# Cached keys stored transposed by page, pages loaded by SyncE at addresses from registers, eight page numbers per register load

## The chip, the cores and the metric

The kernel runs on one core of one Trainium2 chip. The metric is device time in microseconds (us), the lower the better: the median of three runs. A profiled execution of the same program is read beside it.

The engines are named as the profile names them: PE (TensorE, matmuls) with PEld (its weight loads), ACT (ScalarE), DVE (VectorE), POOL (GpSimd) and SP (SyncE, which here only issues DMAs).

## The reference, cut to what matters

One layer of a decoder trunk, for 512 prompt tokens and 8 sample groups of 4 tokens that share the weights. In words and lines of the reference:

```
mod = silu(c) @ w_ada + b_ada                       # six modulation vectors
h   = rmsnorm(x, norm1) * (1 + sc1) + sh1
bg, cg, xin, q, kc, vc, ks, vs, kw, vw, nsa_g, merge_g = split(h @ w_in)
y_a = (bg * conv3(cg * xin)) @ w_out_conv
# sample group: past = 1024 positions in 8 pages of 128, named by page_table
rows(cache) = cache[page_table] + the group's new rows
kc, vc = compress(rows(cache_cmp))    # gelu(blocks of 32 rows @ w1) @ w2, stride 16
o_b = g0 * attend(q, kc, vc) + g1 * attend(q, top 16 blocks of rows(cache_sel))
      + g2 * attend(q, window: cache_win + new rows)       # each with a distance penalty
x   = x + g1 * ((ga * y_a + gb * (o_b @ w_o_nsa)) @ w_out)
x   = x + g2 * SwiGLU(rmsnorm(x, norm2) ...);   y = rmsnorm(x, norm_f)
```

`cache_cmp` and `cache_sel` are 80 physical pages of 128 rows; a row holds the keys and the values of four heads, 512 numbers in all. `cache_win` holds 512 such rows for each of the 8 sample groups ("batches" below). The three attention branches of a sample batch need for their scores the keys with the channel on the partitions, and for their weighted sums the values with the position on the partitions.

## The kernel before, in words

Everything is float32. A product of two float32 matrices is made of three passes over PE: both operands are split into a rounded high part and a rest (weights by `split`, L225: ACT copies the high part at L231, DVE subtracts at L232), and `mm3` (L235) multiplies high by high (L236), high by rest (L237) and rest by high (L238). A token batch of 544 columns is cut in halves of 288 and 256.

Weights come as slabs of 1 MB, loaded by SP (`slab`, L222) into a ring of three buffers, in the order in which they are used. In the first stage the function `queue` ties each SP DMA behind the one issued before it, so that SP works through one list written by hand: page table, first compression weights, the small constants `hp`, the pages of batch 0, and so on. Elsewhere a scheduler that estimates durations places each engine's instructions; an engine then works through its own list strictly in that order.

The stages, in order:

1. **Compression** (to about 151 us of the trace). For each batch `b` and `v` = 0 (keys) or 1 (values), that is `n` = 0 to 15 with `b = n // 2`: `cmp_gather` loads the 8 pages of a batch (one register load of a page number and one DMA each, L464 and L465), `cmp_split` makes the high part on ACT (`xh`, L494) and the rest on DVE (`xl`, L495) of two blocks of 128 x 1024, `cmp_M` runs 48 matmuls (L507 to L509) into the PSUM tile `phi`, `cmp_finish` adds and applies Gelu (`t` on ACT at L515, two DVE additions, `h` on ACT at L519). The splits of step `n + 1` are written behind the finish of step `n`. Between the steps stand the slabs of the modulation weights (`mod_slab`, PE at L285) and the norm of the tokens. Batch 0 is loaded in two goes, keys first, the values behind the second compression weights. `wake` (L539) runs matmuls on constants whose result nobody uses.
2. **Linears for keys, values, gates and queries** (to about 305 us). The queries are written to DRAM (`q_dr`, L733) to be rearranged.
3. **Samples** (about 305 to 526 us). `sample_gen` runs once for each pair of batches: scores on the compressed keys, importance, then `branch` for the selected keys and `branch` for the window. Its instructions are laid between the matmuls of `fill_gen`, 108 quarters of linears with 12 matmuls each, which are needed anyway: `yield k` in `sample_gen` hands over to `k` quarters. One pair yields 27 quarters, four pairs and the start of each 112.

   Within a pair: `gather` loads the selected pages by one indirect DMA per batch on POOL (L820, 2 MB each, tile `sraw`), with row numbers `ixs` that DVE works out from the page table at the end of stage 1; the window comes by two POOL DMAs of 1 MB (`wraw`). The loaded keys have the position on the partitions, so `key_T` (L881) turns them on PE against an identity matrix, four transposes of 128 x 128 into a PSUM tile, and ACT or DVE copies that out (`kt`, L183 or L185). Then `ss` (L900) multiplies queries by keys, `softmax_part` (L810) adds the bias table, ACT takes the exponential (L911), DVE normalises (L917), PE turns the probabilities (`pt`, L924), they are copied out (`pts`), and `sacc` (L931) sums the values.
4. The merge of both mixers, the prompt's attention, the output projection and the FFN (to the end).

The order of a branch in the code, cut:

```
kts = key_T(raw, 0, 0); yield 1; kts += key_T(raw, 0, 1); yield 1
for q4 in range(k): ss matmuls (4 quads); softmax_part; next key_T's with yields
exp, normalise; yield 4
transposes pt and copies pts; yield 1
sacc matmuls
```

Of the kernel before, what the change touches and what calls it, by code (L numbers as in the profile page):

```python
# [142 lines left out]
def build(tc, a, o):  # L143
# [262 lines left out]
    pti = mp.tile([128, 64], I32, name="pti")  # L406
    ptf = mp.tile([128, 64], F32, name="ptf")
    pm_ = mp.tile([128, 64], F32, name="pm_")
    fidx = mp.tile([128, 8], F32, name="fidx")
    queue(lambda: sync.dma_start(pti, a["page_table"].rearrange("(x b) g -> x (b g)", x=1).broadcast_to([128, 64])))  # L410
# [39 lines left out]
    def cmp_gather(b, vs=(0, 1)):  # L450


        if b not in gb_:
            if b == 6:
                gb_[b] = [raw_tile("gt6").rearrange("p (j w) -> p j w", j=4) for _ in range(2)]
            elif b in (2, 5, 7):
                gb_[b] = [gat.tile([128, 8, 512], F32, tag="gt", bufs=1, name=nm("gt"))]
            else:
                gb_[b] = [hpool.tile([128, KC * NT], F32, tag="h" + "hl"[b in (1, 4)], bufs=1, name=nm("gt"))[:, 0:4096].rearrange("p (j w) -> p j w", j=8)]
        cs = slice(256 * vs[0], 256 * vs[-1] + 256)  # L460

        def page(pg):
            t = gb_[b][pg // 4][:, pg % 4, cs] if b == 6 else gb_[b][0][:, pg, cs]
            r = sync.value_load(pti[0:1, b * 8 + pg:b * 8 + pg + 1], min_val=0, max_val=N_PHYS - 1)  # L464
            return sync.dma_start(t, ccv[bass.ds(r, 1)].rearrange("n p w -> (n p) w")[:, cs])  # L465
# [87 lines left out]
    for n in range(16):
# [41 lines left out]
        if n == 15:  # L595
            mk8 = tsm[:, 19:27].rearrange("p (x m) -> p x m", x=1).broadcast_to([128, 8, 8])
            with tc.issue_after(last_lo[0].ins):
                dve.tensor_copy(ptf, pti)
                dve.tensor_mul(pm_.rearrange("p (b x) -> p b x", b=8), ptf.rearrange("p (b x) -> p b x", b=8), mk8)
                dve.tensor_reduce(fidx, pm_.rearrange("p (b x) -> p b x", b=8), axis=AX.X, op=ALU.add)  # L600
                dve.tensor_scalar(ixs, fidx, 16.0, tsm[:, 2:3], ALU.mult, ALU.add)
# [879 lines left out]
```

## Time and profile before

| | before |
|---|---|
| median of 3 runs | 1327.63 us (1326.82 to 1328.21) |
| the profiled execution, its own time | 1327.7 us |
| its span, first to last instruction | 1325.9 us |
| mean granted TensorE clock | 0.988 |
| DMA moved | 191.39 MB, mean 144 GB/s |
| stage 1 up to | 151.5 us |
| stage 2 up to | 305.0 us |
| stage 3 up to | 526.5 us |

The span is what the trace shows; 1.8 us of the execution's own time lie outside it. The stage ends are read from the trace's timeline of PE by the first matmul of the next stage.

How to read what follows. A group row gives the line of the code, the engine, the operation, `out<-in` by the program's names, partitions x elements, a count, and times. A row of the waits view gives who waited for whom, the sum, the number of waits, and the longest. A row of the windows view gives a stretch of the span, its length, the busy time of each engine in it with the number of its instructions, the granted TensorE clock as a share of full speed, the mean share of the DMA engines, and GB/s. A row of the timeline gives a start, a duration, the instruction, and in brackets how long its engine stood idle before it and who released it. `SPq` and `POOLq` are the sequencers that issue DMAs.

### The profile page before, as it was taken

Reading aid. Unit: us, or ns where it says so; the run is one execution under the profiler, and the core shown is the slowest. Engines: PE = TensorE matmul, PEld = TensorE weight load, DVE = VectorE, ACT = ScalarE, POOL = GpSimd, SP = SyncE. Lnnn points to the kernel's source line nnn. Section 1 sums busy time; section 2 is a strip of 40 time slices with the busy share of each in tenths; the row PEclk is TensorE's granted clock in tenths of the full one; section 3 lists DMA queues with packets and bytes.
Section 4 is the critical chain, followed back from the end, with each engine's and each line's share of the span. In section 5 each row is a group of like instructions: output and inputs, shape, how many; then the busy total and the mean of one; then the engine's idle time right before and its main releaser. Section 6 shows DMA issues by size and latency. Waiting matters only on the chain.

```text
span 1325.9 us, 26272 instructions
## 1 busy us (share of the span) xinstructions
PE 1293.4 (98%) x10950; PEld 1208.0 (91%) x10950; DVE 641.5 (48%) x1553; ACT 542.8 (41%) x1070; POOL 54.8 (4%) x105
## 2 busy tenths in 40 slices
PE   6999999999999999999999999999999999999997
PEld 4889999998898998998778778999999999999996
DVE  3347632344355454336668576667333333333335
ACT  4346543333232335126677676445323222222223
POOL 1000120001111010001000000000000000000000
PEclk8899999999999999999999999999999999999998
DMA  5975146663755543834536334331123122122211
GB/s 179 360 251 172 68 145 228 223 210 108 278 210 211 223 159 129 210 120 136 150 128 200 108 103 179 127 128 65 64 70 122 64 96 96 56 88 88 88 65 68
DMA packets 43398, 191.39 MB, mean 144 GB/s; under 512 B 4980, under 2 KB 12532, under 8 KB 26904
## 3 DMA queue, kind: packets, MB, share of 16 engines
q1 hardware_dynamic: 40832, 163.52, 36.6%
q0 software_dynamic: 2448, 26.19, 5.1%
q8 instruction: 86, 1.41, 0.4%
q14 instruction: 32, 0.26, 0.1%
HBM read 174.49 MB, written 23.54 MB: 149 GB/s over the span
## 4 chain that ended last, share of the span: by engine, by line
PE 91%; DMA 3%; SPq 2%; DVE 1%; issue 1%; ACT 1%; POOL 0%; POOLq 0%; DVEq 0%; ACTq 0%
PE lin L236 19%; PE lin L237 19%; PE lin L238 19%; PE dn L238 3%; PE dn L236 3%; PE dn L237 3%; PE acc L1164 3%; PE ptp L1170 3%; PE phi L507 2%; PE modp L285 2%; PE phi L508 2%; PE phi L509 2%; DMA wraw<-in_cache_win 2%; PE kt L881 2%; PE sp L1139 1%
## 5 line engine op out<-in xcount | busy, mean ns | idle before, releaser
L232 DVE TENSOR_TENSOR wl<-raw,wh 128x1024 fp32r<-128x1024 f32 (+1 forms) x148 | 178.7, 1207 | 261.4 <-ACT wh L231 260.9
L231 ACT ACTIVATE wh<-raw 128x1024 fp32r<-128x1024 f32 (+1 forms) x148 | 154.9, 1047 | 332.6 <-PE lin L237 238.7
L236 PE MATMUL lin<-h_h,wh 128*128 128x288 f32 x976 | 286.8, 294 | 0.0
L238 PE MATMUL lin<-h_h,wl 128*128 128x288 f32 x976 | 281.4, 288 | 0.0
L237 PE MATMUL lin<-h_l,wh 128*128 128x288 f32 x976 | 280.9, 288 | 0.0
L237 PE MATMUL lin<-h_lo,wh 128*128 128x288 f32 (+1 forms) x672 | 193.9, 289 | 0.0
L238 PE MATMUL lin<-h_hi,wl 128*128 128x288 f32 (+1 forms) x672 | 193.4, 289 | 0.0
L236 PE MATMUL lin<-h_hi,wh 128*128 128x288 f32 (+1 forms) x672 | 192.7, 287 | 0.0
L236 PEld LDWEIGHTS lin<-h_h,wh 128*128 128x128 f32 x976 | 183.8, 188 | 9.5 <-issue 8.3
L237 PEld LDWEIGHTS lin<-h_l,wh 128*128 128x128 f32 x976 | 183.9, 188 | 0.4
L238 PEld LDWEIGHTS lin<-h_h,wl 128*128 128x128 f32 x976 | 183.7, 188 | 0.3
L236 PEld LDWEIGHTS lin<-h_hi,wh 128*128 128x128 f32 x672 | 126.8, 189 | 0.0
L237 PEld LDWEIGHTS lin<-h_lo,wh 128*128 128x128 f32 x672 | 126.5, 189 | 0.2 <-DVE h_lo L361 0.2
L238 PEld LDWEIGHTS lin<-h_hi,wl 128*128 128x128 f32 x672 | 126.1, 188 | 0.0
L236 PE MATMUL dn<-f_hi,wh 128*128 128x256 f32 (+1 forms) x352 | 101.7, 289 | 0.0
L238 PE MATMUL dn<-f_hi,wl 128*128 128x256 f32 (+1 forms) x352 | 101.5, 288 | 0.0
L237 PE MATMUL dn<-f_lo,wh 128*128 128x256 f32 (+1 forms) x352 | 101.1, 287 | 0.0
L507 PE MATMUL phi<-xh,wph 128*128 128x256 f32 x256 | 77.4, 302 | 9.8 <-ACT xh L494 9.8
L508 PE MATMUL phi<-xl,wph 128*128 128x256 f32 x256 | 75.9, 296 | 3.1 <-DVE xl L495 3.1
L1146 ACT ACTIVATE P<-P,nms 128x512 f32<-128x512 f32 (+3 forms) x128 | 70.7, 555 | 19.6 <-DVE nms L1145 18.7
L509 PE MATMUL phi<-xh,wpl 128*128 128x256 f32 x256 | 75.1, 294 | 0.0
L1145 DVE CUSTOM_DVE_ANT_0 P<-sp,ta 128x512 f32<-128x512 f32 (+3 forms) x128 | 57.6, 482 | 30.1 <-PE sp L1133 22.4
(349 smaller groups left out, 2381.6 us busy)
## 6 DMA issues: line engine op xcount, KB each, us to landing
raw<-in_wt SPq DMA_DIRECT2D x98, 1024.0 KB, 4.9
gt<-in_cache_cmp SPq DMA_DIRECT2D x56, 256.0 KB, 3.2
wraw<-in_cache_win POOLq DMA_DIRECT2D x8, 1024.0 KB, 8.7
out_new_win_sample<-in_cache_win SPq DMA_DIRECT2D x8, 512.0 KB, 5.8
out_new_win_sample<-in_cache_win SPq DMA_DIRECT2D x8, 504.0 KB
raw<-in_wt SPq DMA_DIRECT2D x4, 768.0 KB, 4.2
xT<-in_xT SPq DMA_DIRECT2D x1, 2176.0 KB
x<-in_xT SPq DMA_DIRECT2D x1, 2176.0 KB
```

What stands on the lines that cost most here:

```text
L231: act.activation(oh, view, AF.Copy)
L232: dve.tensor_sub(ol, view, oh.bitcast(F32))
L236: pe.matmul(p, lhsT=wh[:, k, :], rhs=xh, start=start, stop=False)
L237: pe.matmul(p, lhsT=wh[:, k, :], rhs=xl, start=False, stop=False)
L238: pe.matmul(p, lhsT=wl[:, k, :], rhs=xh, start=False, stop=stop)
L507: pe.matmul(ps_, lhsT=w_h, rhs=mh, start=(ch == 0 and s == 0), stop=False)
L508: pe.matmul(ps_, lhsT=w_h, rhs=ml, start=False, stop=False)
L509: pe.matmul(ps_, lhsT=w_l, rhs=mh, start=False, stop=(ch == 7 and s == 1))
L1145: dve.tensor_tensor_reduce(out=t[:, 0:n], in0=sps[br], in1=t_dist[:, 512 - n:512], scale=-hs, scalar=3e38, op0=ALU.add, op1=ALU.min, accum ...
L1146: act.activation(t[:, 0:n], t[:, 0:n], AF.Exp, scale=-1.0, bias=nms[:, c:c + 1], accum_out=sums[:, c:c + 1])
L1164: pe.matmul(acc[br * 64:br * 64 + 64, :], lhsT=vtok[br][:, j, g * 64:(g + 1) * 64], rhs=pts_[br], start=(j == 0), stop=False)
L1170: pe.transpose(tp[:, r * 128:(r + 1) * 128], P[br, r][:, 128 * j:128 * j + 128], ident)
```

## The change

- **The page table** is loaded to one partition (`ptr`, 1 x 64) instead of to all 128 (`pti`).
- **Register loads**: `pages_of` reads the eight page numbers of a batch with one instruction into eight registers and issues eight DMAs behind it, in place of one load, one check and one DMA for each page.
- **Batch 0** of the compression pages comes whole, ahead of the second compression weights. From batch 3 on a batch's pages are put in SP's list ahead of the modulation slab of the same step, at `n` = 1, 3, 5, 8, 11 in place of 2, 4, 6, 8, 11, and the token tile `xT` is asked for at `n` = 2 in place of 1. `wake` runs three matmuls where it ran two, once.
- **Cached keys transposed**: on the host, each page of `cache_sel` and each window is laid out so that the key half has the channel on the rows and the position in the columns; the value half stays. `key_T` with its transposes and copies is gone, `ss` reads the loaded tile. The bias tables take plain position order.
- **Selected pages** are loaded by SP, 16 page DMAs for a pair, instead of by POOL's indirect DMA: the first pair's ahead of the query linears, the next pair's right behind the selected branch's weighted sum. The window is asked for by SP as the pair starts. `sraw` has three buffers where it had two. The row numbers `ixs` are not worked out any more.
- **The yields** of a pair are 4, 3, 6, 2, 5, 5, 2, 2, 2 (31 quarters) where they were 27 in all, so four pairs with their starts hold 128 places for the 108 quarters.

The diff, cut:

```diff
+    def pages_of(b, cache, dst):
+        src = a[cache].rearrange("(n p) w -> n p w", p=128)
+        ld, regs = queue(lambda: nc.values_load_multi_w_load_instructions(ptr[:, b * 8:b * 8 + 8], [mybir.EngineType.SP], ...), lambda r: r[0][-1])
         for pg in range(8):
-            queue(lambda: page(pg))
+            queue(lambda: sync.dma_start(dst(pg), src[bass.ds(regs[pg], 1)].rearrange("n p w -> (n p) w")))
...
-    cmp_gather(0, (0,))
+    cmp_gather(0)
     phi_load(1)
-    cmp_gather(0, (1,))
...
-    wake(2)
+    wake(3)
...
-        for s_ in AHEAD.get(n, ()):
-            adas.append(slab("ada", s_))
-        if n == 1:
+        if n in (1, 3, 5, 8, 11):
+            cmp_gather({1: 3, 3: 4, 5: 5, 8: 6, 11: 7}[n])
+        if n in AHEAD:
+            adas.append(slab("ada", AHEAD[n]))
+        if n == 2:
             queue(lambda: sync.dma_start(xT.rearrange("p k n -> p (k n)"), a["xT"]))
-        if n in (2, 4, 6, 8, 11):
-            cmp_gather({2: 3, 4: 4, 6: 5, 8: 6, 11: 7}[n])
...
+    def gather(bp):
+        rows_of[bp] = [srp.tile([128, 8, 512], F32, tag="sraw", bufs=3, name=nm("sraw")) for _ in range(2)]
+        for b2 in range(2):
+            pages_of(2 * bp + b2, "cache_sel", lambda pg: rows_of[bp][b2][:, pg, :])
+    gather(0)
...
-        sraw = gather(bp)
+        sraw = rows_of.pop(bp)
+        wt = srp.tile([128, 2, 2048], F32, tag="sraw", bufs=3, name=nm("wraw"))
         for b2 in range(2):
+            sync.dma_start(wt[:, b2], a["cache_winT"][b0 + b2])
...
-            kts = key_T(raw, 0, 0)
-            yield 1
-            kts += key_T(raw, 0, 1)
-            yield 1
             for q4 in range(k):
-                for (b2, gp, rows), kt in zip(quads, kts):
-                    pe.matmul(p[rows, :], lhsT=qbd[:, b0 + b2, gp, :], rhs=kt, start=True, stop=True)
+                for b2, gp, rows in quads:
+                    pe.matmul(p[rows, :], lhsT=qbd[:, b0 + b2, gp, :], rhs=keys(b2, gp, q4), start=True, stop=True)
...
-            yield 4
+            yield wait
...
-        yield from branch(sraw, 8, [bs[:, 0:512], bs[:, 512:1024]], 64, 1, True)
-        wt = srp.tile([128, 2, 4, 512], F32, tag="sraw", bufs=2, name=nm("wraw"))
-            pool.dma_start(wt[:, b2], a["cache_win"][b0 + b2].rearrange("(p j) w -> p j w", j=4))
-        yield 6
-        yield from branch(wr, 4, [t_win], 96, 2, False)
+        yield from branch(..., 8, [bs[:, 0:512], bs[:, 512:1024]], 64, 1, True, 6)
+        if bp < 3:
+            gather(bp + 1)
+        yield 5
+        yield from branch(..., 4, [t_win], 96, 2, False, 5)
```

Four places where the instructions stand otherwise. The first is SP's list at the start. `gt_2` is batch 0's tile of pages, `raw_1` and `raw_3` are the two slabs of compression weights, `ISA` rows are register arithmetic. Before:

```order
L410 DMA pti_122<-in_page_table 128x64
L222 DMA raw_1_144<-in_wt 128x2048
L474 DMA hp_134<-in_hp 128x264
L464 TENSOR_LOAD pti_122
L464 ISA x2
L465 ISA
L465 DMA gt_2_147<-in_cache_cmp 128x256
L464 TENSOR_LOAD pti_122
L464 ISA x2
L465 ISA
L465 DMA gt_2_147<-in_cache_cmp 128x256
```

After:

```order
L406 DMA ptr_121<-in_page_table 1x64
L220 DMA raw_1_140<-in_wt 128x2048
L468 DMA hp_130<-in_hp 128x264
L448 TENSOR_LOAD ptr_121
L450 ISA
L450 DMA gt_2_143<-in_cache_cmp 128x512
L450 ISA
L450 DMA gt_2_143<-in_cache_cmp 128x512
```

Before, a page half costs five instructions; after, a whole page costs two, and one load stands ahead of eight pages.

The second place is ACT's list around the steps `n` = 1 to 3. `xh_31` and `xh_33` are the high parts for `n` = 2, `xh_42` and `xh_44` (after: `xh_43` and `xh_45`) for `n` = 3, all from batch 1's tile `gt_4`; `t1_29` belongs to the finish of `n` = 1. Before:

```order
L515 ACTIVATE t1_29_675<-phi_26_619,pbias_136 128x256
L494 ACTIVATE xh_31_681<-gt_4_311 128x1024
L519 ACTIVATE h1_30_679<-t1_29_675 128x252
L494 ACTIVATE xh_33_685<-gt_4_311 128x1024
L494 ACTIVATE xh_42_772<-gt_4_311 128x1024
L494 ACTIVATE xh_44_776<-gt_4_311 128x1024
```

After (`xh_19` and `xh_21` are the high parts for `n` = 1, `t1_17` the finish of `n` = 0):

```order
L487 ACTIVATE xh_19_342<-gt_2_143 128x1024
L487 ACTIVATE xh_21_346<-gt_2_143 128x1024
L423 ACTIVATE wph1_127<-raw_3_169 128x512 x4
L508 ACTIVATE t1_17_336<-phi_15_284,pbias_132 128x256
L512 ACT_TABLE_LOAD
L512 ACTIVATE h1_18_340<-t1_17_336 128x252
L487 ACTIVATE xh_31_433<-gt_4_172 128x1024
L487 ACTIVATE xh_33_437<-gt_4_172 128x1024
L487 ACTIVATE xh_43_549<-gt_4_172 128x1024
L487 ACTIVATE xh_45_553<-gt_4_172 128x1024
L181 ACTIVATE kcs0_89<-ph2_28_423 128x2x63
L508 ACTIVATE t1_29_427<-phi_26_371,pbias_132 128x256
```

The splits for `n` = 1 have moved ahead of the finish of `n` = 0, and those for `n` = 2 and 3 ahead of the finish of `n` = 1. The split for `n` = 6 (`xh_80`), which before stands behind the finish of `n` = 5, has likewise moved ahead of it.

The third place is ACT's list around `n` = 7 and 8. `t1_105` is the finish of `n` = 7, `xh_107` and `xh_109` the high parts for `n` = 8 from batch 4's tile. After:

```order
L508 ACTIVATE t1_93_976<-phi_91_921,pbias_132 128x256
L512 ACTIVATE h1_94_980<-t1_93_976 128x252
L508 ACTIVATE t1_105_1055<-phi_103_1002,pbias_132 128x256
L487 ACTIVATE xh_107_1061<-gt_62_673 128x1024
L487 ACTIVATE xh_109_1065<-gt_62_673 128x1024
```

Before, the same `xh_107` stands two rows ahead of `t1_105`; now it stands behind it.

The fourth place is PE's list near the end of the samples: `pt` and `sacc` of the last pair's selected branch, `ss` of its window, and `lin`, the fill. Before, fill follows the transposes `pt`:

```order
L924 MATMUL pt_759_6405<-ident_66,S_726_6198 128x128 x4
L924 MATMUL pt_761_6412<-ident_66,S_726_6198 128x128 x4
L236 MATMUL lin_767_6426<-h_h_2076,wh_765_6422 128x288
L237 MATMUL lin_767_6426<-h_l_2077,wh_765_6422 128x288
L238 MATMUL lin_767_6426<-h_h_2076,wl_766_6423 128x288
```

After, with the last fill matmul as the first row:

```order
L236 MATMUL lin_688_5918<-h_h_1553,wl_686_5889 128x256
L876 MATMUL ss_695_5992<-wraw_654_5717,qbd_95 32x512
L895 MATMUL pt_689_5944<-ident_66,S_676_5859 128x128 x4
L895 MATMUL pt_691_5951<-ident_66,S_676_5859 128x128 x4
L876 MATMUL ss_695_5992<-wraw_654_5717,qbd_95 32x512 x3
L902 MATMUL sacc_675_5858<-sraw_619_5364,pts_690_5949 32x128 x2
```

Behind these rows no fill stands any more: the rest of the selected sum, the window's `pt`, `ptx`, `sacc` and `ot` follow one upon the other up to the linears of the merge. SP's list has the 16 page DMAs of `gather(0)` right behind the last query slab and ahead of the writes to `q_dr` and of the next two slabs; the 16 of each later pair stand ahead of one to two slabs of the fill and wait for the `sacc` that frees their buffers.

More of the change, by code (lines that the diff above doesn't have):

```diff
@@ L206, in build, with queue @@
     ordered, last_q = [True], [None]
-    def queue(f):
+    def queue(f, ins=lambda r: r):
         if not ordered[0]:
@@ L403, in build @@
     v_dr = [dr.tile([128, 1024], F32, name=f"v_dr{j}") for j in range(2)]
[L406 to L410, printed above, removed]
+    ptr = mp.tile([1, 64], I32, name="ptr")
+    ptv = a["page_table"].rearrange("(x b) g -> x (b g)", x=1)
+    queue(lambda: sync.dma_start(ptr, ptv))
     p0 = ExitStack()
@@ L445, in build, with cmp_gather @@
     gat = mkpool(gst, "gat", side="right")
-    ccv = a["cache_cmp"].rearrange("(n p) w -> n p w", p=128)
     gb_ = {}
[L450 to L465, printed above, removed]
-        for pg in range(8):
-            queue(lambda: page(pg))
+    def pages_of(b, cache, dst):
+        src = a[cache].rearrange("(n p) w -> n p w", p=128)
+        ld, regs = queue(lambda: nc.values_load_multi_w_load_instructions(ptr[:, b * 8:b * 8 + 8], [mybir.EngineType.SP], min_val=0, max_val=N_PHYS - 1, skip_runtime_bounds_check_because="a page table names pages of the cache"), lambda r: r[0][-1])
+        for pg in range(8):
+            queue(lambda: sync.dma_start(dst(pg), src[bass.ds(regs[pg], 1)].rearrange("n p w -> (n p) w")))
+    def cmp_gather(b):
+        if b == 6:
+            ts = [raw_tile("gt6").rearrange("p (j w) -> p j w", j=4) for _ in range(2)]
+        elif b in (2, 5, 7):
+            ts = [gat.tile([128, 8, 512], F32, tag="gt", bufs=1, name=nm("gt"))]
+        else:
+            ts = [hpool.tile([128, KC * NT], F32, tag="h" + "hl"[b in (1, 4)], bufs=1, name=nm("gt"))[:, 0:4096].rearrange("p (j w) -> p j w", j=8)]
+        gb_[b] = ts
+        pages_of(b, "cache_cmp", lambda pg: ts[pg // 4][:, pg % 4] if b == 6 else ts[0][:, pg])
     xst = ExitStack()
@@ L595, in build @@
         if n == 15:
[L596 to L601, printed above, removed]
             xst.close()
@@ L813, in small @@
         return smp.tile([128, w_], F32, tag=f"sm_{n}", bufs=2, name=nm(n))
[L816 to L822 removed]
     def sample_gen(bp):
         b0 = 2 * bp
[L827 removed]
+        sraw = rows_of.pop(bp)
+        wt = srp.tile([128, 2, 2048], F32, tag="sraw", bufs=3, name=nm("wraw"))
+        for b2 in range(2):
+            sync.dma_start(wt[:, b2], a["cache_winT"][b0 + b2])
         quads = [(b2, gp, slice(b2 * 64 + gp * 32, b2 * 64 + gp * 32 + 32)) for b2 in range(2) for gp in range(2)]
@@ L869, in sample_gen, with branch @@
         for jh in range(2):
[L870 to L872 removed]
+            pool.tensor_tensor(bs[:, jh * 512:(jh + 1) * 512].rearrange("p (s k) -> p s k", s=8),
+                               t_sel[:, jh * 512:(jh + 1) * 512].rearrange("p (s k) -> p s k", s=8),
+                               mk[:, jh * 8:jh * 8 + 8].rearrange("p (s y) -> p s y", y=1).broadcast_to([128, 8, 64]), op=ALU.add)
         dve.tensor_scalar_mul(px[:, 0:63], px[:, 0:63], G[:, 0:1])
[L875 to L885 removed]
+        yield 3
         acc = acc_ps(nm("sacc"))
[L889 removed]
+        def branch(keys, vals, nj, tables, xo, br, first, wait):
             S = smp.tile([128, 1024], F32, tag="S", bufs=1, name=nm("S"))
```

77 lines of the change are left out of this document (30 added, 47 removed).

## The prediction

> **What bounds the kernel now.** I read the page first.
>
> ```profile
> span 1325.9 us, 26272 instructions
> PE 1293.4 (98%) x10950; PEld 1208.0 (91%) x10950; DVE 641.5 (48%) x1553; ACT 542.8 (41%) x1070; POOL 54.8 (4%) x105
> PEclk8899999999999999999999999999999999999998
> ```
>
> PE is busy for 98% of the span, so a change pays only if it takes matmuls off PE, removes one of its few idle stretches, or keeps its clock up. The clock row is low in the first two slices only. I therefore cut the span by windows, small ones at the start, where the change moves loads.
>
> ```profile
> 11.80:17.40 5.60, 0.06 (x2) 0.04 (x1) 0.67 (x3) 1.15 (x2) 0.00 (x0) 0.71 0.59 200
> 17.40:28.50 11.10, 10.09 (x82) 9.51 (x82) 5.76 (x11) 3.55 (x7) 0.00 (x0) 0.69 0.54 174
> 28.50:33.00 4.50, 1.97 (x9) 1.35 (x10) 2.09 (x4) 3.72 (x5) 0.00 (x0) 0.80 0.81 237
> 33.00:40.70 7.70, 7.70 (x47) 7.56 (x45) 0.51 (x1) 0.00 (x0) 0.00 (x0) 0.68 0.91 325
> 40.70:44.00 3.30, 0.92 (x5) 0.65 (x5) 2.23 (x4) 3.20 (x5) 0.00 (x0) 1.00 0.89 294
> 44.00:48.20 4.20, 4.20 (x47) 3.68 (x46) 3.00 (x3) 1.64 (x3) 0.00 (x0) 0.60 0.81 296
> 48.20:75.80 27.60, 27.60 (x300) 25.53 (x299) 7.76 (x18) 7.85 (x15) 0.00 (x0) 1.00 1.01 390
> 75.80:80.00 4.20, 1.13 (x6) 0.91 (x5) 2.50 (x4) 3.75 (x9) 0.00 (x0) 0.88 0.94 331
> 80.00:82.50 2.50, 2.50 (x37) 1.80 (x36) 2.29 (x4) 2.15 (x4) 0.00 (x0) 0.53 0.96 338
> 82.50:151.50 69.00, 69.00 (x651) 65.55 (x650) 50.20 (x132) 43.59 (x83) 0.31 (x4) 1.00 0.42 138
> 305.00:526.50 221.50, 216.17 (x2060) 197.69 (x2059) 110.78 (x291) 77.70 (x135) 26.12 (x55) 1.00 0.49 187
> 526.50:1325.90 799.40, 788.22 (x6413) 737.27 (x6410) 398.92 (x995) 334.01 (x713) 7.43 (x11) 1.00 0.34 110
> ```
>
> The compression stage has four holes, before 17.4, at 28.5, 40.7 and 75.8 us, and behind each the clock is down (0.69, 0.68, 0.60, 0.53): a hole is paid twice. The sample stage (305 to 526.5) idles for only 5.3 us; what can be had there is PE's own work. Nothing in the last 800 us is touched, and I leave them as they are. The waits of PE name the holes:
>
> ```profile
> PE phi L507 <- ACT xh L494: 9.8, 4, 5.5
> PE phi L508 <- DVE xl L495: 3.1, 4, 0.9
> PE kt L881 <- DMA wraw<-in_cache_win: 2.7, 3, 1.3
> ```
>
> Four waits for the split of cached pages and three for the window.
>
> **The first matmul.** SP's own rows, the chain's row of the page table, and ACT and PE at the start:
>
> ```profile
> L464 SPq TENSOR_LOAD <-pti x72: 263/268/476, 5.0 to 120.5; - x72
> L465 SPq DMA_DIRECT2D gt<-in_cache_cmp x72: 332/333/1219, 6.0 to 121.3; - x72
> 6.01 8.26 SPq L465 DMA_DIRECT2D gt<-in_cache_cmp  x8
> 16.25 2.00 ACT L494 ACTIVATE xh<-gt 128x1024 fp32r<-128x1024 f32 x2 [4.64 <-DMA gt<-in_cache_cmp]
> 17.36 0.58 PE L507 MATMUL phi<-xh,wph 128*128 128x256 f32 x1 [5.54 <-ACT xh L494]
> ```
>
> Eight half pages take 8.26 us to issue, a period of about 1.1 us, of which the DMA instruction is 0.33. The last is issued at 14.3 and the split starts at 16.25, 2.0 later. After the change a page costs the DMA and one or two small register operations, I say 0.4 us; eight are out 3.2 us after the first. They are whole pages now, 2 MB, and at the 390 GB/s of the window 48.20 to 75.80 that takes 5.4 us: from 6.3, with 2.0 for the landing, ready at 13.7. That is 2.6 ahead of 16.25. One register load for eight numbers is not in the trace: between one load as now (0.27) and eight of them (2.1). I take the short end, since one instruction replaces eight, and with the bounds of the transfer get **-2.6 (-4 to -1)**. [...]
>
> The clock in 17.4 to 28.5 is 0.69, so 3.4 us are lost there. The hole before shrinks from both sides (one more `wake` matmul, the earlier data), to some 3 us: I take **-1.5 (-3.4 to 0)**.
>
> **The three holes that go.** At 28.5 the split of batch 0's values stands behind the finish of step 0, because the values come in a second go. After, the split's two ACT rows stand ahead of that finish, and the tile is loaded with the keys. Idle 4.50 - 1.97 = 2.5, and 7.70 us at 0.68 lose 2.5: **-5.0 (-5.6 to 0)**. At 40.7 the split for step 2 stands behind the finish of step 1 in ACT's list:
>
> ```profile
> 40.80 0.47 ACT L515 ACTIVATE t<-phi,pbias 128x256 f32<-128x256 f32 x1 [8.57 <-PE phi L509]
> ```
>
> ACT had idled 8.57 us before it, and the split could have run there. After, batch 1's four splits stand ahead. Idle 3.30 - 0.92 = 2.4, and 4.20 at 0.60 lose 1.7: **-4.1**. At 75.8 the same for step 6: idle 3.1, 2.50 at 0.53 lose 1.2: **-4.3**. The cover for all three is that the pages land in time. In bytes, batch 3's pages (needed by step 6) stand after 12 MB of SP's list, some 31 us at 390 GB/s, so at about 37; step 6 starts near 60. Batch 1's end after 6.2 MB, at about 22 us, and step 2 starts near 28.
>
> **One new hole.** The split of batch 4 for step 8 now stands behind the finish of step 7 on ACT. It is the shape of the holes at 40.7 (4.1) and 75.8 (4.3), so **+4.0 (0 to +5)**.
>
> **The transposes.**
>
> ```profile
> L881 PE MATMUL kt<-ident,sraw x128: 270/273/331, 309.8 to 489.3; 128*128 128x128 f32 x128
> L881 PE MATMUL kt<-ident,wraw x64: 270/272/301, 341.4 to 514.6; 128*128 128x128 f32 x64
> 309.91 1.90 PE kt L881 x16
> 317.01 0.87 PE kt L881 x8
> ```
>
> The 270 ns are a pipelined matmul's full length; what PE is held for is read from the chain of waits, 1.90 for 16 or 0.87 for 8, that is 0.119 or 0.109 each. PE is full here, so all 192 count: 22.8 (20.9 to 22.8). **-22.8**. The copies on ACT and DVE that fall away, the index arithmetic on DVE and POOL's DMAs lie beside PE: 0. `ss` reads its 512 columns as four pieces of 128 where it read one; the `phi` matmuls, which read pieces of 32 columns, run 300 in 27.60 us with the rest of that window, so 0. The window's load is asked for at the start of the pair, and the three waits of the third view go: **-2.7**. Nothing waits next: `ss` has its keys long before, and the four score blocks still wait for DVE's `mk` and POOL's table as before.
>
> **The end of the samples.** 128 places are handed over for 108 quarters, so the fill ends within the fourth pair, and what follows is a chain. The end before:
>
> ```profile
> 518.56 0.72 ACT L911 ACTIVATE S<-S,m 128x512 f32<-128x512 f32 x1 [0.96 <-DVE m L909]
> 520.31 0.48 DVE L917 TENSOR_SCALAR S<-S,f 128x512 f32<-128x512 f32 x1
> 521.93 0.60 PE L924 MATMUL pt<-ident,S 128*128 128x128 f32 x4
> 522.01 1.06 ACT L231 ACTIVATE wh<-raw 128x1024 fp32r<-128x1024 f32 x1 [2.33 <-PE lin L237]
> 522.57 0.69 DVE L185 COPY pts<-pt 128x512 f32<-128x512 f32 x1 [1.62 <-PE pt L924]
> 523.31 1.08 PE L931 MATMUL sacc<-wraw,pts 128*32 128x128 f32 x32 [0.67 <-DVE pts L185]
> 523.36 1.28 ACT L1022 ACT_TABLE_LOAD   x1
> 524.65 0.66 ACT L1022 ACTIVATE ga<-ga 128x544 f32<-128x544 f32 x1
> 525.53 0.33 PE L953 MATMUL ot<-ident,ob 128*128 128x128 f32 x1 [0.92 <-ACT ob L950]
> 526.49 0.72 PE L236 MATMUL lin<-yin_hi,wh 128*128 128x288 f32 x3
> ```
>
> From `pt` at 521.93 to the next linear at 526.49 are 4.6 us, in which PE works about 2.7. After, ACT's list behind the last fill is: split 1.06, copy 0.4, table 1.28, sigmoid 0.66, copy of `pts` 0.6, table 1.28, exponential 0.72; then from its end to the normalised `S` 1.5, and `pt`, `pts`, `sacc`, the output 3.5 to 4.2: some 11.7 us. PE has in it, beside the 2.7, the selected branch's `pt`, `sacc` and one `ss` that stood among the fill: 1.2 + 2.2 + 1.0, so 7. Idle 4.7 against 1.9 makes +2.8, and a hole of that length costs 1.2 to 2 us of clock, as after 75.8 and 40.7. **+4.5 (+2 to +9)**; the far end is the hole with both table loads bare and the clock down for longer.
>
> **SP's queue.** The 16 pages of a later pair wait for the `sacc` that frees their buffers, and a slab of the fill stands behind them. Between the `sacc` and the use of that slab I count 304 matmuls; at 799.40 / 6413 = 0.125 each that is 38 us, less the slab's landing and split, 7: 31 us of cover for pages of 0.4 each, 6.4. So 0, and 0 (to +3) for the `q_dr` writes behind `gather(0)`, since `linear` has further buffers.
>
> **Sum**: -2.6 - 1.5 - 5.0 - 4.1 - 4.3 + 4.0 - 22.8 - 2.7 + 4.5 = -34.5. The profiled execution's own time is 1327.7 (span 1325.9 and 1.8 outside), within 0.1 of the median 1327.63, so **1293 us**.
>
> **The rivals.**
>
> A: The pages come no faster, and the holes of the first stage stay. The windows 11.80 and 17.40 moved 200 and 174 GB/s while pages were the load; if that is the rate of small pieces and not of their issue, batch 0 whole needs 10 us and more, and the splits wait for data instead of for ACT's list. Then only transposes, window, the new hole, the end of samples and at most the first term are left: -22.8 - 2.7 + 4.0 + 4.5 - 2.6 = -19.6, so **1308**. [...] Against it, the window 48.20 moved 390 GB/s with pages in the mix. Chance 0.12.
>
> B: The two new holes don't show, as step 8 finds other work of PE and the exponential is off the end: -34.5 - 8.5 = -43, so **1284.5**. For it, PE has modulation matmuls about step 8, and in the trace of before step 4 crosses without a hole. Chance 0.12.
>
> C, slower: SP's one queue. The pages of a later pair hold the slabs back. It decides where 16 pages take over 31 us, 1.9 each; each further us is paid three times (pairs 2 to 4). To be slower than before it must make up 34.5, 11.5 each time, so 2.7 us a page; at 2.75 it is 3 x 13 = 39, **1332**. The nearest row:
>
> ```profile
> 47.79 14.30 SPq L465 DMA_DIRECT2D gt<-in_cache_cmp  x8
> ```
>
> Eight issues took 14.3, 1.8 each, where the DMA engines were full (390 GB/s); in the sample stage they are at 0.49. Chance 0.04.
>
> **How the numbers follow.** My forecast has 0.72, A 0.12, B 0.12, C 0.04. The forecast's own range, from the bounds of the terms (first term +1.6, clock +1.5, end +4.5 upward; new hole -4, end -2.5, clock -1.9 downward, not all at once), is 1286 to 1300. B lies just below and A above; 1281 to 1305 leaves out A, C and the edges, below 2 in 10. What a measurement of this kernel can tell from no change is 0.2%, 2.7 us; every case but C is far under that. Faster 0.95, same 0.02 (C near its point of balance), slower 0.03.
>
> **What would show it.** In the profile after: the first `phi` near 14.7; no wait of `phi` for `xh` at steps 1, 2 and 6, one of 2 to 3 us at step 8 with a low clock behind it; no `kt`; 16 pages issued in 6 to 8 us; PE's busy time lower by about 25; stage 3 shorter by about 21, a hole of several us near its end; the stretch behind it unchanged at 799. It is wrong if the holes of stage 1 stay with ACT waiting for `gt`, if `lin` waits for splits that wait for `raw`, or if the register load takes several us.

## The result, and the profile after

| | before | after |
|---|---|---|
| median | 1327.29 us (4 runs, 1326.82 to 1328.21) | 1294.78 us (4 runs, 1293.24 to 1294.94) |
| the profiled execution, its own time | 1327.7 us | 1294.94 us |
| its span | 1325.9 us | 1293.2 us |
| mean granted TensorE clock | 0.988 | 0.992 |
| PE busy | 1293.4 us | 1269.4 us |

The ratio is 0.9752, with a 95% interval of 0.9735 to 0.9769. The forecast was 1293, in a range of 1281 to 1305. The total is met within 2 us, but by luck: two misses of opposite sign cancel, as the stages show. I cut both spans at the same three instructions: the first linear behind the compression, the first score of the samples (`sx`), and the first matmul on `yin`, the merge's input, which ends the samples. The middle two stretches of before:

```profile
151.50:301.50 150.00, 150.00 (x1230) 148.74 (x1228) 51.50 (x87) 54.18 (x89) 16.80 (x24) 1.00 0.55 190
301.50:526.49 224.99, 219.66 (x2099) 201.04 (x2097) 112.00 (x291) 79.02 (x137) 26.79 (x56) 1.00 0.49 187
```

After, with the starts of the first stage and the holes in rows of their own (the columns are those of the windows in the prediction):

```profile
8.00:13.30 5.30, 3.77 (x38) 1.79 (x38) 1.59 (x5) 2.92 (x6) 0.00 (x0) 1.00 1.06 415
13.30:22.30 9.00, 8.12 (x62) 7.90 (x66) 7.19 (x9) 4.89 (x7) 0.00 (x0) 0.81 1.03 405
22.30:30.00 7.70, 7.70 (x106) 7.32 (x98) 4.26 (x7) 5.96 (x7) 0.00 (x0) 1.00 1.04 407
30.00:71.80 41.80, 41.78 (x431) 39.36 (x423) 17.99 (x35) 17.38 (x36) 0.00 (x0) 1.00 0.82 326
71.80:74.70 2.90, 0.54 (x2) 0.34 (x3) 1.93 (x4) 2.88 (x5) 0.00 (x0) 1.00 0.00 0
74.70:80.00 5.30, 5.30 (x94) 4.34 (x95) 5.10 (x10) 4.18 (x11) 0.00 (x0) 1.00 0.39 140
...
133.86:284.60 150.74, 150.74 (x1231) 149.43 (x1230) 51.54 (x88) 53.87 (x90) 15.68 (x22) 1.00 0.58 198
284.60:487.18 202.58, 199.08 (x1905) 182.07 (x1905) 97.84 (x268) 66.84 (x114) 13.94 (x42) 0.99 0.57 210
487.18:491.26 4.08, 0.63 (x7) 0.41 (x4) 1.99 (x4) 2.91 (x6) 0.00 (x0) 0.86 0.32 106
491.26:497.00 5.74, 5.74 (x24) 5.74 (x25) 4.39 (x7) 0.00 (x0) 0.00 (x0) 0.50 1.03 261
```

| stage | before | after | measured | forecast |
|---|---|---|---|---|
| compression, to the first linear | 151.5 | 133.9 | -17.6 | -13.5 |
| linears, to the first `sx` | 150.0 | 150.7 | +0.7 | 0 |
| samples, to the first matmul on `yin` | 225.0 | 202.6 | -22.4 | -21.0 with the row below |
| the rest | 799.4 | 806.0 | +6.6 | |
| sum | 1325.9 | 1293.2 | -32.7 | -34.5 |

The first stage gave 4 us more than I said. The transposes and the window's wait were to bring -25.5 in the samples; -22.4 came there and +6.6 went behind them, so the end of the samples cost 9.7 (what is left when those 25.5 are taken as right), where I said 4.5 and 9 at most. PE's waits in the changed kernel:

```profile
PE lin L235 <- DVE yin_lo L265: 3.5, 1, 3.5
PE phi L500 <- ACT xh L487: 3.0, 2, 1.5
PE pt L895 <- DVE S L888: 2.5, 1, 2.5
PE phi L501 <- DVE xl L488: 1.7, 2, 0.9
```

Of the four waits for `xh` two are left, the first matmul and step 8; the window's is gone. The second row from the bottom is the hole that I forecast at the end of the samples. The first row I had not forecast at all. The timeline of DVE and PE there:

```profile
486.30 0.80 DVE L931 COPY o_s<-ot 64x32 f32<-64x32 f32 x4 [3.00 <-PE ot L925]
487.12 0.68 DVE L966 COPY nco<-ncp 18x512 f32<-18x512 f32 x1
487.18 0.63 PE L234 MATMUL lin<-yin_hi,wh 128*128 128x288 f32 x3
489.89 0.68 DVE L966 COPY nco<-ncp 18x512 f32<-18x512 f32 x1 [2.09 <-DMA out_new_conv_sample<-nco]
491.26 0.61 PE L235 MATMUL lin<-yin_lo,wh 128*128 128x288 f32 x1 [3.45 <-DVE yin_lo L265]
```

DVE's second copy into `nco` (the convolution's new state on its way to DRAM) waits for the DMA that empties the first, and `yin_lo`, which the merge's first linear needs, stands behind it. In the kernel before, seven of the eight `yin_lo` stood ahead of that second copy:

```profile
527.33 4.51 DVE L267 TENSOR_TENSOR yin_lo<-yinf,yin_hi 128x544 fp32r<-128x544 f32 x7
531.78 0.67 DVE L994 COPY nco<-ncp 18x512 f32<-18x512 f32 x1
```

After, PE idles 3.45 us, and then 5.74 us run at a clock of 0.50. Behind the first hole, the wait for `S`, the clock is down as well:

```profile
482.00:487.18 5.18, 4.13 (x54) 3.07 (x53) 1.70 (x7) 1.73 (x4) 0.00 (x0) 0.67 0.19 75
```

From 476 to 497 us PE idles 6.95 us, where it idled 2.1 from 520 to 530 before; the two stretches of low clock lose about 1.4 and 2.9 us (work at 0.67 and at 0.50), where before the clock was 1.00. Counted in this way, the end costs about 9.1 us more.

At the start, the rows of SP, ACT and PE that answer to those of before, with the register load of eight page numbers:

```profile
L448 SPq TENSOR_LOAD <-ptr x16: 525/529/1740, 2.0 to 431.5; - x16
2.99 4.03 SPq L450 DMA_DIRECT2D gt<-in_cache_cmp  x8
12.20 3.90 ACT L487 ACTIVATE xh<-gt 128x1024 fp32r<-128x1024 f32 x4 [2.37 <-DMA gt<-in_cache_cmp]
13.31 0.39 PE L500 MATMUL phi<-xh,wph 128*128 128x256 f32 x1 [1.54 <-ACT xh L487]
```

The first page is asked for at 2.99, not at 6.0, because the narrow page table is there by 2.0; the first `phi` comes 4.05 us earlier, where I said 2.6.

### The profile page after: what moved, and what is told of

The parts are those of the page before. It is cut to its first block, busy times and chain, and to the rows that moved or that the text cites. A ratio compares the mean times of both kernels' runs of the same rounds, so it can differ in the third digit from the quotient of the medians.

```text
span 1293.2 us, 25776 instructions
## 1 busy us (share of the span) xinstructions
PE 1269.4 (98%) x10760; PEld 1187.6 (92%) x10760; DVE 627.1 (48%) x1525; ACT 531.3 (41%) x1048; POOL 40.9 (3%) x89
## 4 chain that ended last, share of the span: by engine, by line
PE 96%; DVE 2%; ACT 1%; DMA 1%; SPq 0%; issue 0%; ACTq 0%; DVEq 0%
PE lin L234 20%; PE lin L235 20%; PE lin L236 20%; PE dn L236 3%; PE dn L234 3%; PE dn L235 3%; PE acc L1136 3%; PE ptp L1142 3%; PE phi L500 3%; PE phi L501 2%; PE phi L502 2%; PE modp L283 2%; PE sp L1111 1%; PE sp L1112 1%; PE sacc L902 1%; PE ss L876 1%
## 5 line engine op out<-in xcount | busy, mean ns | idle before, releaser
L500 PE MATMUL phi<-xh,wph 128*128 128x256 f32 x256 | 74.7, 292 | 3.0 <-ACT xh L487 3.0
L1117 DVE CUSTOM_DVE_ANT_0 P<-sp,ta 128x512 f32<-128x512 f32 (+3 forms) x128 | 57.6, 482 | 30.0 <-PE sp L1105 22.4
## 6 DMA issues: line engine op xcount, KB each, us to landing
xT<-in_xT SPq DMA_DIRECT2D x1, 2176.0 KB, 13.3
```

The source lines that it names most:

```text
L500: pe.matmul(ps_, lhsT=w_h, rhs=mh, start=(ch == 0 and s == 0), stop=False)
L1117: dve.tensor_tensor_reduce(out=t[:, 0:n], in0=sps[br], in1=t_dist[:, 512 - n:512], scale=-hs, scalar=3e38, op0=ALU.add, op1=ALU.min, accum ...
```

## The experiments

Theory 1 is the prediction's mechanism, mended for what the profile after showed: holes of the first stage follow ACT's order and the landing of batch 0; PE's transposes are the bulk; the end of the samples costs because the fill has run out and because of `nco`. Each experiment but the last two makes one change to the changed kernel (1294.78), though 5 brings a second buffer with it and 10 moves the token tile too. The kernel before was timed again beside each group of runs: its median was 1329.14 us beside 1 to 4, 1328.12 beside 5 to 8 and 1328.41 beside 9 to 12, where it was 1327.29 beside the changed kernel. So each "more" or "less" against 1294.78 is uncertain by 1 to 2 us, and where it is no larger than 2 to 3 us the profiles carry the argument.

**1. Two buffers for `nco`.**

```diff
-        nco = cv.tile([18, 512], F32, tag="nco", bufs=1, name=nm("nco"))
+        nco = cv.tile([18, 512], F32, tag="nco", bufs=2, name=nm("nco"))
```

> The tile nco (the convolution's new state on its way out) has two buffers instead of one; the rest is the changed kernel. Theory 1: behind the samples DVE's second copy into nco waits for the output DMA of the first, and the split yin_lo of the merge's first linear stands behind it on DVE; PE waits 3.5 us and then runs 5.7 us at half clock. With two buffers both go: about 1294.8 - 3.5 - 2.9 = 1288.4, and no wait of lin for yin_lo over 1 us. Rival: DVE would be late anyway, because the fill has run out and o_s, nco and yin_lo come one upon the other; then PE still waits 2 to 3 us and the clock still drops: 1293 to 1295.

Measured: 1294.88 (1294.71 to 1295.72), no change. Theory 1 failed in its remedy. The timeline of DVE in this run, and the wait of PE:

```profile
487.28 1.28 DVE L966 COPY nco<-ncp 18x512 f32<-18x512 f32 x2
490.16 3.27 DVE L265 TENSOR_TENSOR yin_lo<-yinf,yin_hi 128x544 fp32r<-128x544 f32 x5 [1.60 <-DMA out_new_conv_sample<-nco]
490.94 0.61 PE L235 MATMUL lin<-yin_lo,wh 128*128 128x288 f32 x1 [2.99 <-DVE yin_lo L265]
```

The two copies now follow one another, and `yin_lo` itself waits for the output DMA. My reading is that its tile is allotted where `nco` lay, since the pool of `nco` is closed just ahead of it; the trace shows the wait, not the addresses. The wait has moved by one instruction and is nearly as long (2.99 us, where it was 3.45). The time is the rival's, its reason is not: DVE is done with both copies and idles 1.60 us for the DMA.

**2. Fill up to the end.** 26 quarters for a pair instead of 31.

```diff
-        yield 3
+        yield 2
...
-                          8, [bs[:, 0:512], bs[:, 512:1024]], 64, 1, True, 6)
+                          8, [bs[:, 0:512], bs[:, 512:1024]], 64, 1, True, 5)
...
-        yield 5
+        yield 4
...
-        yield 2
+        yield 1
...
-        yield 2
+        yield 1
```

> The yields of a pair are 4, 2, 5, 2, 4, 5, 2, 1, 1, 26 in all, so four pairs and the start hand over 108 places for the 108 quarters of the fill; the rest is the changed kernel, nco with one buffer. Theory 1: the tail of the samples costs because the fill has run out. With fill up to the end the wait of pt for S (2.5 us) goes and the clock stays full up to the last pt: 3 to 4.5 us less, 1290.5 to 1292; the wait of yin_lo behind nco stays at 3 us or so. Rival: places are only moved, and the chain of the last pair's window branch costs the same wherever it ends, with shorter waits for each of several stops: 1294 to 1296.

Measured: 1287.43 (1287.18 to 1287.61), 7.4 less than the changed kernel. The wait of `pt` for `S` is gone from PE's waits; of the other hole this is left, with the only stretch of low clock at the end of the samples:

```profile
PE lin L235 <- DVE yin_lo L265: 2.5, 1, 2.5
...
PE lin L234 <- ACT yin_hi L264: 1.1, 1, 1.1
```

```profile
485.00:487.00 2.00, 2.00 (x8) 2.00 (x9) 2.00 (x4) 0.55 (x1) 0.00 (x0) 0.50 0.91 227
487.00:489.00 2.00, 2.00 (x12) 2.00 (x12) 2.00 (x4) 0.00 (x0) 0.00 (x0) 0.67 1.01 256
```

Theory 1 holds and was priced too low. From 475 to 489 us PE idles 3.7 us, 3.3 less than in the changed kernel; and the clock loses about 1.7 us here, where it lost 1.4 and 2.9 there. Together that is some 6 of the 7.4; the rest is not traced.

**3. The split for step 8 first.**

```diff
-        fin_ = cmp_finish(b, v, po)
-        if n < 15:
+        if n == 7:
+            xs_ = [cmp_split(4, 0, hc) for hc in range(2)]
+            with tc.issue_after(last_hi[0].ins):
+                fin_ = cmp_finish(b, v, po)
+        else:
+            fin_ = cmp_finish(b, v, po)
+        if n < 15 and n != 7:
```

> The split of batch 4's pages for step 8 stands ahead of the finish of step 7 in ACT's list; the rest is the changed kernel. Theory 1: the hole at step 8 (71.8 to 74.7 us, 2.4 us idle, the clock full) comes from ACT's order alone: it goes, 1292.4, and phi waits for xh only once, at the start. Rival: the pages or the buffers of the split are what is late: the hole stays and the time is 1294.8.

Measured: 1291.77 (1290.39 to 1292.14), 3.0 less. PE waits for `xh` only once:

```profile
PE phi L500 <- ACT xh L487: 2.1, 1, 2.1
```

Nothing but this split was moved, and the pages come as before: the order made the hole, not the landing of the pages.

**4. Batch 0 in two goes.**

```diff
-    cmp_gather(0)
+    cmp_gather(0, slice(0, 256))
     phi_load(1)
+    cmp_gather(0, slice(256, 512))
```

> Batch 0 of the cached pages comes in two goes again, keys ahead of the second compression weights and values behind them, each go with one register load; the rest is the changed kernel. Theory 1: whole loading is what removes the hole at step 1, about 5 us with its clock; with two goes the values land some 3 us later and in ACT's list the second split for step 2 falls behind the finish of step 1, so that a hole of 2 to 3 us and half a clock period come back: 1297 to 1300. Rival: the faster issue alone is enough, the values land by 14 us, ahead of the end of step 0 near 22: 1293 to 1295.

Measured: 1295.21 (1293.71 to 1297.51), no difference that can be told. The rival holds: the hole at step 1 does not come back. Less is loaded ahead of the first split, so PE starts 2.3 us earlier and keeps its clock (its matmuls follow 0.12 us apart from 12.5 to 18.0 us, where those of the changed kernel stand 0.21 apart from 15.8 to 19.0); this is paid back by 0.8 to 1.1 us of waiting for `xl` at four steps, where the changed kernel has two such waits, and by the hole at step 8, which now costs clock as well:

```profile
11.03 0.44 PE L503 MATMUL phi<-xh,wph 128*128 128x256 f32 x1
...
72.35 0.39 PE L503 MATMUL phi<-xh,wph 128*128 128x256 f32 x1 [1.51 <-ACT xh L490]
73.61 0.58 PE L504 MATMUL phi<-xl,wph 128*128 128x256 f32 x1 [0.88 <-DVE xl L491]
```

```profile
74.00:78.00 4.00, 4.00 (x42) 3.08 (x42) 2.53 (x5) 2.49 (x5) 0.00 (x0) 0.50 0.00 0
```

**5. The convolution's state early.** The lines that write `nco` out, in a function, called ahead of the fourth pair, with two buffers.

```diff
     for bp in range(4):
+        if bp == 3:
+            new_conv()
         for n in sample_gen(bp):
```

> The transposes of the convolution's new state, its two copies nco (two buffers) and their output DMAs are moved from behind the last pair to ahead of the fourth pair's start; the rest is the changed kernel. Theory 1: what holds yin_lo is the memory of nco, first as DVE's second copy behind the first one's DMA, and with two buffers as yin_lo's own memory, which lies over that of nco; with the DMAs done long before, the wait of 3.5 us goes but for 1 us or less, and with it the half clock of 5.7 us (2.9 lost): 1288 to 1290. Rival: DVE is late anyway behind o_s, since ACT's yin_hi starts only at 485.6: wait of 2 us or more and the clock as before, 1293 to 1295.

Measured: 1291.22 (1290.08 to 1293.45), 3.6 less, where I expected 4.8 to 6.8. The wait for `yin_lo` shrinks as theory 1 said:

```profile
PE lin L235 <- DVE yin_lo L265: 0.7, 1, 0.7
```

```profile
487.00:500.00 13.00, 12.55 (x87) 12.56 (x88) 7.41 (x12) 3.85 (x7) 0.00 (x0) 0.87 0.74 179
```

Not all of the clock comes back (0.87 over 13 us is 1.7 lost), and the wait of `pt` just ahead is still there. That `yin_lo` was held by the output DMAs of `nco` is shown by this run and the first together; that it is by their memory remains the reading of run 1.

**6. The transposes put back, without the copies.**

```diff
+                for b2, gp, rows in quads:
+                    tp = tp_ps(nm("kt"))
+                    kk = keys(b2, gp, q4)
+                    for j in range(4):
+                        pe.transpose(tp[:, j * 128:(j + 1) * 128], ..., ident)
                 p = s_ps(nm("ss"))
```

> The 192 transposes of 128 x 128 on PE are put back ahead of the score matmuls, four into each PSUM tile, but nobody copies the tiles out or reads them (keys are used as loaded, so no result changes): the price of the transposes alone, without the copies. Theory 1: PE is full, each holds it 0.109 to 0.119 us: 20.9 to 22.8 us, less up to 3 us for those of the fourth pair that fall into the hole at the end: 1313 to 1318, and no new wait. Rival: most of what the samples gained came from elsewhere (order of the fill, loads, freed ACT and DVE), and bare transposes cost 10 us or less: 1300 to 1305.

Measured: 1316.69 (1315.20 to 1318.18), 21.9 more. That is 0.114 us for each of 192, between the 0.109 and 0.119 of the prediction's rows. The wait of `pt` at the end also grew, from 2.5 to 3.4 us, so a little of the 21.9 is not the transposes' own. Theory 1 holds, and little is left for the freed copies on ACT and DVE.

**7. Page numbers one by one** (for the compression pages).

```diff
+        if cache == "cache_cmp":
+            def page(pg):
+                r = sync.value_load(ptr[0:1, b * 8 + pg:b * 8 + pg + 1], min_val=0, max_val=N_PHYS - 1)
+                return sync.dma_start(dst(pg), src[bass.ds(r, 1)].rearrange("n p w -> (n p) w"))
+            for pg in range(8):
+                queue(lambda: page(pg))
+            return
```

> The page numbers of the compression pages are loaded one by one again, each with its bounds check and its DMA behind it; the selected pages keep the eight-number loads; the order of the loads is that of the changed kernel. Theory 1: SP's issue of a page goes from 0.5 to about 1.1 us; batch 0's last page is issued at 3 + 8.3 = 11.3 instead of 7.0, so the first split starts some 1 us later (13.3 instead of 12.2); later batches have their pages long before use: 1295 to 1297. Rival: the slow issue is what made the holes at steps 1, 2 and 6: with 1.1 us a page they come back, 5 us and more: 1300 to 1308.

Measured: 1297.19 (1296.58 to 1298.30), 2.4 more. Theory 1 holds in kind and just misses in size: the first `phi` is 2.3 us later, where I expected 1. This delay, and not the time alone, is the evidence.

```profile
3.07 8.25 SPq L451 DMA_DIRECT2D gt<-in_cache_cmp  x8
...
15.65 0.39 PE L508 MATMUL phi<-xh,wph 128*128 128x256 f32 x1 [2.94 <-ACT xh L495]
```

The holes at steps 1, 2 and 6 did not come back with the slow issue.

**8. The page table on 128 partitions.**

```diff
-    ptr = mp.tile([1, 64], I32, name="ptr")
+    ptr = mp.tile([128, 64], I32, name="ptr")
-    queue(lambda: sync.dma_start(ptr, ptv))
+    queue(lambda: sync.dma_start(ptr, ptv.broadcast_to([128, 64])))
```

> The page table is loaded to 128 partitions again, in place of one; the rest is the changed kernel. Theory 1: the first page DMA stood at 3.0 us in the changed kernel and at 6.0 before because the narrow table lands 2.9 us earlier (register load at 2.0 against 5.0); with the wide one the pages start near 6, the first phi comes 1.5 to 3 us later, near 15 to 16: 1296.3 to 1298. Rival: the table's landing does not matter, since the weights slab and the pages are bound by the transfer; first phi at 13.3, 1294.8.

Measured: 1297.92 (1296.94 to 1299.03), 3.1 more, as theory 1 said. The pages start 3.4 us later, and so does PE:

```profile
6.38 3.97 SPq L450 DMA_DIRECT2D gt<-in_cache_cmp  x8
...
16.72 0.58 PE L500 MATMUL phi<-xh,wph 128*128 128x256 f32 x1 [4.33 <-ACT xh L487]
```

**9. Every selected page twice**, to double what SP's queue holds ahead of other work. The bytes double with it.

```diff
             pages_of(2 * bp + b2, "cache_sel", lambda pg: rows_of[bp][b2][:, pg, :])
+            pages_of(2 * bp + b2, "cache_sel", lambda pg: rows_of[bp][b2][:, pg, :])
```

> Every page of selected keys is loaded twice into the same place, so SP issues 32 page DMAs for a pair instead of 16 and the pages move twice the bytes; the rest is the changed kernel. Theory 1: the queue of SP has cover, 31 us by the prediction's count against the 9.6 to 10.0 us that 16 issues take in the changed kernel; with 32, about 20 us, still covered: 1294 to 1296. Rival (the prediction's C): the cover is smaller than counted, the slabs behind the pages come late, lin waits for splits that wait for raw: each missing us is paid three times, 1300 to 1320.

Measured: 1314.57 (1311.72 to 1317.53), 19.8 more. I was wrong; the rival's mechanism is there, but its place is another one. SP, DVE and PE in the stage of the linears:

```profile
235.35 24.16 SPq L450 DMA_DIRECT2D sraw<-in_cache_sel  x32
266.34 0.48 DVE L729 SCALAR_TENSOR_TENSOR ql<-lin,hd,qh 128x256 fp32r<-128x256 f32 x1 [9.38 <-DMA q_dr0l<-ql]
267.27 0.55 PE L234 MATMUL lin<-h_h,wh 128*128 128x256 f32 x1 [9.35 <-DVE qbd L733]
```

The pages of the first pair hold the writes of the queries to `q_dr`; the tile `ql` is not emptied, DVE waits, no PSUM comes free, and PE stands for 9.35 us. The same rows of the changed kernel, without doubling:

```profile
235.09 12.90 SPq L450 DMA_DIRECT2D sraw<-in_cache_sel  x16
...
255.63 0.48 DVE L728 SCALAR_TENSOR_TENSOR ql<-lin,hd,qh 128x256 fp32r<-128x256 f32 x1 [5.01 <-DMA q_dr0l<-ql]
```

DVE waits 5.0 us there already, and PE just does not feel it: 11.3 us more of SP brought a wait of 9.35, so the cover left is about 2 us. The writes are issued only when the pages are out (at 259.90, where it was 248.09), so they are held by their place in SP's list. But the DMA engines are full as well while the pages go out (a share of 1.01 in the changed kernel, from 235.1 to 248.1 us), so the run does not tell whether the number of DMAs or their bytes sets those 24 us. Of the later pairs, one shows the rival's own place, a slab that comes late behind 32 pages (`lin` waits 2.3 us for `wh`, the weights' split). By the stages of this profile the linears are 11.6 us longer and the samples 8.5; of these 8.5 I did not trace more than that wait and the 4.2 us, for 2.5, that `pt` waits for `S`.

**10. Pages behind the slabs again.**

```diff
-        if n in (1, 3, 5, 8, 11):
-            cmp_gather({1: 3, 3: 4, 5: 5, 8: 6, 11: 7}[n])
...
-        if n == 2:
+        if n == 1:
             queue(lambda: sync.dma_start(xT.rearrange("p k n -> p (k n)"), a["xT"]))
+        if n in (2, 4, 6, 8, 11):
+            cmp_gather({2: 3, 4: 4, 6: 5, 8: 6, 11: 7}[n])
```

> The cached pages of batches 3 to 5 are put behind the modulation slabs again, a step later (2, 4, 6 in place of 1, 3, 5), and the token tile is asked for at step 1; the rest is the changed kernel. In ACT's list the split for step 6 then stands behind the finish of step 5, and the one for step 8 ahead of the finish of step 7. Theory 1: the holes follow ACT's order: the one at step 8 goes (-2.4, and what it may cost in clock), one of 2.5 to 3 us at step 6 comes (with 1 to 1.5 of clock): 1294 to 1297, phi waits for xh near 60 us and not near 73. Rival: the pages' place in SP's queue is itself worth something, as they land too late behind the slabs: ACT waits for gt, and 1298 or more.

Measured: 1296.16 (1294.15 to 1298.75), 1.4 more in the median, with runs that overlap the changed kernel's; as a ratio to the kernel before, timed beside it, 0.9750 where the changed kernel has 0.9752. The time does not differ, then, but the hole goes from step 8 to step 6:

```profile
62.00:65.00 3.00, 1.53 (x5) 1.11 (x5) 2.42 (x3) 3.00 (x7) 0.00 (x0) 0.70 1.01 387
65.00:72.00 7.00, 7.00 (x64) 6.52 (x64) 4.76 (x10) 3.33 (x7) 0.00 (x0) 0.64 0.52 164
72.00:76.00 4.00, 4.00 (x37) 3.79 (x36) 0.83 (x3) 1.26 (x3) 0.00 (x0) 1.00 0.04 12
```

Past 72 us PE is full, where the changed kernel has its hole. ACT's row of the split for step 6:

```profile
61.49 2.00 ACT L487 ACTIVATE xh<-gt 128x1024 fp32r<-128x1024 f32 x2
```

It follows the finish of step 5 at once and has waited for no page. Theory 1 holds: the place in SP's queue acts through ACT's order. That the scheduler draws this order up by when it believes the pages to be there is my reading; no run shows it.

**11 and 12. Three mends together** (2, 3 and 5, the state written from within the fourth pair, where its convolutions are done), with batch 0 whole, and with batch 0 in two goes.

```diff
-        yield 5
+        yield 4
+        if bp == 3:
+            new_conv()
         yield from branch(lambda b2, gp, q4: wt[:, b2, gp * 512:(gp + 1) * 512],
```

> Three mends in one on the changed kernel: 26 quarters for a pair (as in the run with the fill to the end), the split for step 8 ahead of the finish of step 7, and the convolution's state written from within the fourth pair (two buffers of nco). Theory 1: the gains add, since they lie at different places: 1294.8 - 7.4 (fill) - 3.0 (split) - 2.5 to 4 (the wait of yin_lo that the fill run still had, 2.5, with its clock): 1280.5 to 1282. Rival: removing one hole uncovers the next (yin_hi on ACT, clock periods elsewhere): 1283 to 1286.

> The same three mends, and batch 0's pages in two goes, keys first. Theory 1: in the run with two goes the first phi came 2.3 us earlier and the clock stayed up behind it; what it lost was a hole at step 8 with its clock, which is mended here: 2 to 3 us below the run with batch 0 whole, 1278 to 1280. Rival: the splits of steps 1 and 2 wait for data and half a step each is given back: no difference to the other run.

Measured: 1283.30 (1283.21 to 1284.81) and 1283.24 (1281.33 to 1284.02); against before 0.9658 (0.9642 to 0.9674) and 0.9655 (0.9639 to 0.9671). Both beat both kernels. The mends do not add: 7.4, 3.0 and 3.6 would make 14.0, and 11.5 came. In both the rival holds. In the first, these waits are left at the end of the samples:

```profile
PE lin L234 <- ACT yin_hi L264: 1.5, 1, 1.5
...
PE lin L235 <- DVE yin_lo L265: 0.8, 1, 0.8
```

In the second the first `phi` comes at 12.11, where it comes at 13.54 in the first, and two waits at step 2, 1.97 us together, take this back:

```profile
27.09 0.38 PE L503 MATMUL phi<-xh,wph 128*128 128x256 f32 x1 [1.10 <-ACT xh L490]
28.35 0.39 PE L504 MATMUL phi<-xl,wph 128*128 128x256 f32 x1 [0.87 <-DVE xl L491]
```

## Why the prediction was right, and where it was not

- **The transposes, -22.8**: right. Run 6 gives 21.9 for putting them back, inside the range of 20.9 to 22.8.
- **The window's wait, -2.7**: gone from the waits of PE.
- **The first matmul, -2.6**: mis-sized, -4.05, by two errors of opposite sign. I kept the first page at 6.0 us and priced the narrow table at nothing; it was asked for at 2.99, which is 3.0 of the 4.05. And from the first page's issue to the split I counted 7.7 us (6.0 to 13.7), where 10.2 passed before; 9.2 were measured (2.99 to 12.20), so faster issue and whole loading gave 1.0 and not 2.6. The rate of 390 GB/s was not too high: the window of 8 to 13.3 moved 415. Likely the slab of weights that stands ahead of the pages in SP's list took its share, which I left out; that is not traced. Run 8 puts the first `phi` 3.4 us later for the wide table, run 7 2.3 for the single loads; their times, 3.1 and 2.4 more, lie too close to rank the two. The load of eight registers, which I put between 0.27 and 2.1 us and took at the short end, takes 0.53 us in the median, twice the single load's 0.27.
- **The clock behind it, -1.5**: 9.00 us at 0.81 lose 1.7 where 3.4 were lost, so -1.7.
- **The holes at steps 1, 2 and 6, -13.4**: gone. The reason given for step 1, that whole loading was needed, is too narrow: neither two goes (run 4) nor slow issue (run 7) alone brings it back; both together were not run. The hole at step 6 comes back with the old order (run 10), as the prediction has it. No run brings back those at steps 1 and 2, so what removed them is argued from ACT's list and not shown.
- **The new hole at step 8, +4.0**: it is there, with 2.4 us idle, but the clock stays at 1.00 behind it. Its cause is ACT's order (run 3). In run 4 a hole of the same length costs clock, 0.50 for 4 us. So the length alone does not decide whether the clock drops; what does, no run shows.
- **The end of the samples, +4.5 (to +9)**: the step that failed in size; it measured 9.7 as the remainder and about 9.1 counted in the trace. The first hole, for `S`, came as described, with its two small waits behind it 3.5 us idle and about 1.4 of clock. The second, `yin_lo` behind `nco` and its output DMA, I had not looked for: DVE's order there had changed too. It cost 3.45 idle and about 2.9 of clock. Run 2 takes the first away, run 5 the second but for 0.7 us, run 11 both but for 0.8.
- **SP's queue, 0**: right in value, with wrong working. Pages take 0.6 us each for the later pairs and 0.8 for the first, not 0.4. For the first pair I named further buffers as cover without a number; run 9 puts the cover left at about 2 us. For the later pairs I counted 31 us; with 32 pages in about 22 us one slab of three already comes late, so it was too many.
- **Rival A** (pieces of 256 KB move slowly) falls: three windows between 8 and 30 us with pages in the mix moved 405 to 415 GB/s, with slabs of 1 MB among them, so whole pages are not held to the 200 and 174 GB/s of the two windows before. **Rival B** falls, as both new holes show. **Rival C** is real as a mechanism and was 2 us away, at another place.

## What to carry to other kernels

Where a change frees time on the engine that bounds the kernel, look at once at where the filler work runs out, and read every engine's order there, not only the one that the change moves: here a copy that waits for an output DMA slipped ahead of a split that PE needs, and PE stood 3.45 us for it, with 5.74 us of half clock behind; run 5, without this wait, is 3.6 us faster. A move in a DMA queue can act through the order of instructions on another engine rather than through the landing of the data: in run 10 a hole went from step 8 to step 6, and the split there had waited for no page. To learn how much cover a queue has left, double what it holds: the first wait that shows tells the place and the margin (run 9: 11.3 us more of SP, 9.35 of waiting, about 2 of cover).

## What the runs showed of the hardware that was not expected

- A page table of 64 numbers on one partition allows the first register load at 2.0 us; broadcast to 128 partitions, the first page is asked for at 6.4 us (run 8) against 3.0.
- One register load of eight numbers takes 0.53 us in the median, one of a single number 0.27.
- Pages of 256 KB from SP's queue, several in flight and with slabs of 1 MB among them, moved 405 to 415 GB/s in the three windows of the changed kernel between 8 and 30 us.
- An idle stretch of 2.4 us at step 8 left the clock at 1.00 in the changed kernel, and one of the same length brought 4 us at 0.50 in run 4.
